# Feed-forward operands scaled by 1/rms once, and more weight pairs by seven half-block products

## The chip, the cores and the metric

The kernel runs on one core of a Trainium2 chip. The metric is the device time of one execution in microseconds (us), as the median of several runs. One further execution was profiled.

## The reference, cut to what matters

The program is a decoder trunk of two layers on 512 tokens of width 1024. Each layer is a feed-forward half step, a mixing block (attention and a gated MLP, not touched here) and a second feed-forward half step; a last norm ends it.

```
def rmsnorm(x, g):
    y = xf * lax.rsqrt(jnp.mean(xf * xf, axis=-1, keepdims=True) + EPS)
    return y * g
def swiglu(h, w_gate_up, w_down):
    g, u = jnp.split(h @ w_gate_up, 2, axis=-1)      # 1024 x 5632
    return (jax.nn.silu(g) * u) @ w_down             # 2816 x 1024
...
for l in range(DEPTH):                               # DEPTH = 2
    x = x + 0.5 * swiglu(rmsnorm(x, ffn1_norm[l]), ...)
    ...                                              # mixing block
    x = x + 0.5 * swiglu(rmsnorm(x, ffn2_norm[l]), ...)
```

All of it is float32.

## The kernel before

**Precision.** Every float32 operand is split into a high and a low part in the format that TensorE multiplies (fp32r): ScalarE copies it to the high part, VectorE subtracts to get the low part (`split`, line 352). A product is then three matmuls: high by high, high by low, low by high (`chain`, line 380). x is kept transposed, as eight tiles of 128 features by 512 tokens.

**The feed-forward** (`ffn`, line 577, four calls, here FFN1 to FFN4) walks over 22 pairs of weight blocks, j = 0 to 21: 128 gate columns and 128 up columns, each 1024 deep. The pairs come in four chunks, 0 to 5, 6 to 11, 12 to 17 and 18 to 21; after each chunk the down-projection of its hidden tiles runs (eight outputs of 128, 18 matmuls each for a chunk of six).

**A plain pair** (`pair_plain`) is 2 outputs x 8 depth blocks x 3 matmuls = 48 matmuls of 512 columns. **A pair of seven** (`pair_seven`) sees the same product as 2 x 2 blocks (gate and up; the two halves of the depth; the two halves of the tokens) and makes seven block products instead of eight, with sums of blocks as operands, as Strassen and Winograd have it: 7 x 4 depth blocks x 3 = 84 matmuls of 256 columns. It needs sums of the weights (tile `S`, three VectorE instructions per pair) and sums of the tokens' operands (`norm_sums`, line 420: n1, n2, t3, t4, once per feed-forward and depth block q, split into the tiles `Th` and `Tl`), and puts the results together on VectorE (tile `TT`, in the buffer YB). `SEVEN` (line 31) says which pairs do so: two of every three, from j = 4 in FFN1 and from j = 3 in the others, below 21: 11 pairs in FFN1, 12 in FFN2 to FFN4, 47 in all.

**The norm.** The operands `xh`, `xl` are x times the gain only. 1/rms (tile `rbc`, copied from PSUM by VectorE in `norm_finish`) is known later, so the results are multiplied by `rbc`: two VectorE instructions in a plain pair, two GpSimd instructions in a pair of seven. GpSimd also multiplies silu(gate) by up in both.

**Buffers.** Split weights live in a ring of three units of 1024 columns (Fhi in WH, Flo in WL). A plain pair takes two units, a pair of seven three (blocks 11 and 12; s1 and s2; s4 and s3) and half a unit for block 22 (in VH and VL). With the units named by age, a pair of seven finds its first unit free when the pair before has used its first product blocks, its last one when that pair ends. `norm_sums` writes through one buffer `T32`, so one q must be split before the next is summed. The tiles `Th`, `Tl` lie in buffers RB6 to RB11 and VH.

**Order.** The whole program is recorded first (`Recorder`); `order` then puts each engine's instructions in a fixed sequence by a list schedule with estimated costs, lowest index first among what is ready; weight loads and splits count as 100 places earlier (AHEAD). All instructions are issued by one line, 276, so in the profile they are told apart by tile names.

Of the kernel before, what the change touches and what calls it, by code (L numbers as in the profile page):

```python
# [29 lines left out]

def SEVEN(j, begins):

    return j % 3 < 2 and (FIRST if begins else LATER) <= j < 21


NEG = -1e30
# [243 lines left out]
def trunk(ctx: ExitStack, tc, d):  # L280
# [25 lines left out]

    for tag, places, cols, dtype in (
            ("Xraw", [(W[0], 0), (W[1], 0)], 2048, F32), ("Fraw", units(W[0], W[1]), 1024, F32),
            ("S", [(W[2], 0)], 2048, F32), ("T32", [(W[3], 0)], 1024, F32), ("Txa", [(W[4], 0)], S, F32), ("Txb", [(W[4], 512)], S, F32), ("ss0", [(W[4], 1536)], S, F32),
            ("Fhi", units(*WH), 1024, F32R), ("Flo", units(*WL), 1024, F32R),  # L310
            ("F22h", halves(V[1])[:2], S, F32R), ("F22l", halves(V[1])[2:], S, F32R),
            ("raw", units(W[0], W[1])[:3], 1024, F32), ("whi", units(*WH), 1024, F32R), ("wlo", units(*WL)[:2], 1024, F32R),
            ("raw5", units(W[0], W[1])[:3] + units(W[3]), 1024, F32), ("wlo3", units(*WL), 1024, F32R),
            ("whi5", units(*WH, RB[0], RB[1]), 1024, F32R), ("wlo5", units(*WL, RB[2], RB[3]), 1024, F32R),
            ("U", [(W[2], 0)], 2048, F32), ("pA", halves(W[3]), S, F32), ("pB", halves(W[4]), S, F32),
            ("ga", halves(W[1])[2:] + [(G, 0)], S, F32), ("diagh", [(WL[2], 0)], S, F32R), ("diagl", [(WL[2], 512)], S, F32R)):
        rec.over(tag, places, cols, dtype)
# [31 lines left out]
    def f(ap):  # L349
        return ap.bitcast(F32)  # L350
# [43 lines left out]
    def norm_begin(gidx):  # L394
        st["g"] = gains[:, gidx * KD:(gidx + 1) * KD]
        st["xh"], st["xl"] = [None] * KD, [None] * KD
        st["Th"], st["Tl"] = [None] * 4, [None] * 4
        st["s"] = None

    def norm_square(k):  # L400
# [10 lines left out]
    def norm_operand(k):  # L411
# [5 lines left out]
        act(xh, x[:, k, :], AF.Copy, scale=g)  # L417
        vec.scalar_tensor_tensor(xl, x[:, k, :], g, f(xh), op0=ALU.mult, op1=ALU.subtract)

    def norm_sums(q):  # L420

        t, xa, xb = rec.tile("T32", [P, 1024]), rec.tile("Txa", [P, S]), rec.tile("Txb", [P, S])
        act(xa, x[:, q, :], AF.Copy, scale=st["g"][:, q:q + 1])
        act(xb, x[:, q + 4, :], AF.Copy, scale=st["g"][:, q + 4:q + 5])
        n1, n2, t3, t4 = (t[:, n * 256:(n + 1) * 256] for n in range(4))
        vec.tensor_tensor(n1, xa[:, 0:256], xa[:, 256:512], op=ALU.subtract)
        vec.scalar_tensor_tensor(n2, xb[:, 256:512], -1.0, n1, op0=ALU.mult, op1=ALU.subtract)
        vec.tensor_tensor(t3, xb[:, 256:512], xa[:, 256:512], op=ALU.subtract)
# [82 lines left out]
        nb[0] += 1  # L511
        return bank(nb[0] % 6, "ps_gu")

    def pair_plain(w):
        out = []
        for p, q in (("21", "22"), ("11", "12")):
            ps = next_bank()
# [5 lines left out]
            chain(ps, ops)  # L523
            out.append(ps)
        g, u = tt("g"), tt("u")
        vec.tensor_tensor(g, out[0], rbc, op=ALU.mult)
        act(g, g, AF.Silu)
        vec.tensor_tensor(u, out[1], rbc, op=ALU.mult)
        pool.tensor_tensor(u, u, g, op=ALU.mult)
        return u  # L530

    def pair_seven(w):

        xh, xl, Th, Tl = st["xh"], st["xl"], st["Th"], st["Tl"]

# [18 lines left out]
        A, B, C, D = (next_bank() for _ in range(4))  # L554
        s1, TT = tt("s1")[:, 0:256], rec.tile("TT", [P, 1024])
        L, R = TT[:, 0:512], TT[:, 512:1024]
        times(A[:, 0:256], "11", "11")
        act(s1, A[:, 0:256], AF.Copy)
        times(B[:, 0:256], "12", "21")
        times(B[:, 256:512], "s2", "n2")  # L560
        vec.tensor_tensor(half(L), half(B), two(s1), op=ALU.add)
        times(C[:, 0:256], "s4", "22")
        times(C[:, 256:512], "s3", "t3")
        vec.tensor_tensor(half(R), half(C), two(L[:, 256:512]), op=ALU.add)
        times(D[:, 0:256], "22", "t4")
        vec.tensor_tensor(L[:, 256:512], D[:, 0:256], R[:, 256:512], op=ALU.add)
        times(A[:, 256:512], "s1", "n1")
# [657 lines left out]
```

## Time and profile before

| what | value |
|---|---|
| median of 3 runs | 2169.31 us (2168.56 to 2169.37) |
| the profiled execution: time, span | 2171.32 us, 2169.4 us |
| TensorE (PE) matmuls busy | 2139.0 us, 99% of the span |
| VectorE (DVE), ScalarE (ACT), GpSimd (POOL) busy | 70%, 47%, 17% |
| mean granted TensorE clock | 0.996 of 2.4 GHz |

The span runs from the first instruction to the last; the time has some 2 us around it. Busy shares are means over unlike stages: VectorE's 70% is far higher in some stretches. A matmul's row shows its own length, and matmuls overlap, so the pace of TensorE is read from the starts of successive ones.

### The profile page before, as it was taken

The numbers are of one execution on the slowest core, as the hardware profiler recorded it, in microseconds if no ns is written. First come the engines' busy times: TensorE is split into PE (matmuls) and PEld (weight loads), VectorE is DVE, ScalarE is ACT, GpSimd is POOL, SyncE is SP. The second block draws the span as 40 slices with busy tenths as digits, with TensorE's granted clock in tenths as the row PEclk, the third lists the DMA queues.
The fourth block names the chain that finished last, engine by engine and source line by source line (L and its number), as shares of the span: only waits on it lengthen the run. The fifth ranks groups of instructions, "written<-read, shape, count | busy, mean of one in ns | idle before, by whom it ended". The sixth has DMA issues, their size and how long they took to land.

```text
span 2169.4 us, 30061 instructions
## 1 busy us (share of the span) xinstructions
PE 2139.0 (99%) x11704; PEld 1849.9 (85%) x11704; DVE 1518.8 (70%) x2357; ACT 1011.9 (47%) x1635; POOL 379.6 (17%) x261
## 2 busy tenths in 40 slices
PE   8999999999999999999999999999999999999998
PEld 6898987888878889898888988878888788898986
DVE  7685767678885757585685775685888758585764
ACT  6343334676653533343453433357766436343434
POOL 2131322010000122231311413210100001231411
PEclk9999999999999999999999999999999999999999
DMA  5323333421113323323333232234111233323232
GB/s 191 115 88 107 91 100 114 149 62 47 59 59 124 104 89 106 109 88 107 89 100 113 88 115 87 91 109 160 49 58 50 69 107 97 112 86 114 85 101 68
DMA packets 65664, 209.25 MB, mean 96 GB/s; under 512 B 7793, under 2 KB 8305, under 8 KB 65521
## 3 DMA queue, kind: packets, MB, share of 16 engines
q1 hardware_dynamic: 65520, 207.32, 30.7%
q8 instruction: 92, 1.51, 0.3%
q14 instruction: 52, 0.42, 0.1%
HBM read 205.19 MB, written 2.10 MB: 96 GB/s over the span
## 4 chain that ended last, share of the span: by engine, by line
PE 93%; DVE 4%; ACT 2%; issue 1%; DMA 0%; SPq 0%; DVEq 0%; ACTq 0%
PE b L276 93%; DVE W L276 1%; DVE RB L276 1%; DVE WL L276 1%; DVE xl L276 1%; DVE x L276 1%; ACT WH L276 0%; ACT xh L276 0%; DMA x<-in_x_dram 0%; ACT t L276 0%; ACT L276 0%; ACT RB L276 0%; DVE t L276 0%; DVE YB L276 0%; DVE sm L276 0%
## 5 line engine op out<-in xcount | busy, mean ns | idle before, releaser
L276 ACT ACTIVATE WH<-W 128x1024 fp32r<-128x1024 f32 (+4 forms) x458 | 446.5, 976 | 636.5 <-PE b L276 553.4
L276 DVE TENSOR_TENSOR WL<-W,WH 128x1024 fp32r<-128x1024 f32 (+4 forms) x458 | 528.8, 1157 | 185.1 <-ACT WH L276 122.4
L276 PE MATMUL b<-xh,WH 128*128 128x512 f32 (+1 forms) x1716 | 608.5, 359 | 10.2 <-ACT xh L276 9.3
L276 PE MATMUL b<-xl,WH 128*128 128x512 f32 (+1 forms) x1716 | 608.5, 358 | 0.0
L276 PE MATMUL b<-RB,WH 128*128 128x512 f32 (+2 forms) x2270 | 579.7, 349 | 0.4
L276 PE MATMUL b<-xh,WL 128*128 128x512 f32 (+1 forms) x1716 | 568.8, 358 | 1.4 <-DVE WL L276 1.4
L276 PEld LDWEIGHTS b<-RB,WH 128*128 128x128 f32 x2270 | 397.9, 189 | 57.0 <-DVE x L276 2.1
L276 PE MATMUL b<-RB,WL 128*128 128x512 f32 (+1 forms) x1276 | 391.5, 341 | 0.0
L276 PEld LDWEIGHTS b<-xh,WH 128*128 128x128 f32 x1716 | 326.3, 190 | 56.6 <-ACT xh L276 9.7
L276 PEld LDWEIGHTS b<-xl,WH 128*128 128x128 f32 x1716 | 326.1, 190 | 45.5 <-DVE xl L276 1.1
L276 PEld LDWEIGHTS b<-xh,WL 128*128 128x128 f32 x1716 | 315.8, 190 | 46.6 <-DVE WL L276 2.3
L276 POOL TENSOR_TENSOR YB<-YB,rbc 128x512 f32<-128x512 f32 x94 | 168.6, 1812 | 671.3 <-DVE YB L276 671.3
L276 PEld LDWEIGHTS b<-RB,WL 128*128 128x128 f32 x1276 | 231.7, 190 | 27.3
L276 DVE SCALAR_TENSOR_TENSOR x<-b,x 128x512 f32<-128x512 f32 (+1 forms) x145 | 99.5, 686 | 166.6 <-PE b L276 166.6
L276 PE MATMUL b<-VH,WH 128*128 128x256 f32 (+1 forms) x426 | 136.3, 321 | 4.9 <-DVE W L276 4.9
L276 ACT ACTIVATE RB<-t 128x512 fp32r<-128x512 f32 (+3 forms) x120 | 67.7, 574 | 124.4 <-POOL t L276 112.5
L276 DVE TENSOR_TENSOR t<-b,rbc 128x512 f32<-128x512 f32 (+1 forms) x90 | 61.3, 687 | 91.6 <-PE b L276 91.3
L276 PE MATMUL b<-RB,RB 128*128 128x512 f32 (+4 forms) x478 | 124.8, 346 | 0.0
L276 POOL TENSOR_TENSOR t<-t,t 128x512 f32<-128x512 f32 x41 | 65.6, 1601 | 315.5 <-DVE t L276 253.0
L276 POOL TENSOR_TENSOR W<-W,t 128x512 f32<-128x512 f32 x35 | 49.3, 1409 | 403.0 <-ACT t L276 402.7
L276 DVE TENSOR_TENSOR RB<-t,RB 128x512 fp32r<-128x512 f32 (+3 forms) x120 | 77.0, 649 | 48.2 <-ACT RB L276 47.8
L276 DVE TENSOR_TENSOR W<-W 128x1024 f32<-128x1024 f32 (+3 forms) x87 | 97.7, 1122 | 5.6 <-ACT W L276 2.7
(161 smaller groups left out, 2443.7 us busy)
## 6 DMA issues: line engine op xcount, KB each, us to landing
W<-in_gu_dram SPq DMA_DIRECT2D x176, 512.0 KB, 3.7
W<-in_dn_dram SPq DMA_DIRECT2D x96, 384.0 KB, 3.1
W<-in_wA_dram SPq DMA_DIRECT2D x48, 512.0 KB, 3.5
W<-in_phi_dram SPq DMA_DIRECT2D x16, 512.0 KB, 4.5
W<-in_dn_dram SPq DMA_DIRECT2D x32, 256.0 KB, 2.7
W<-in_wo_dram SPq DMA_DIRECT2D x16, 512.0 KB, 3.5
W<-in_wv_dram SPq DMA_DIRECT2D x8, 512.0 KB, 4.2
W<-in_wu_dram SPq DMA_DIRECT2D x8, 512.0 KB, 5.3
```

Of the source, the lines that this page charges most:

```text
L276: getattr(self.real[engine], op)(*args, **kw)
```

## The change

1. `SEVEN` takes in j = 5 to 20 without a gap, and 3 (FFN2 to FFN4; 4 is plain) or 4 (FFN1; 5 is plain). These are 16 pairs in FFN1 and 17 in the others, 67 in all.
2. After pair 0, `norm_scaled` makes x times gain (ScalarE) times `rbc` (GpSimd) for all eight tiles, into eight buffers `xn`. `norm_sums` sums those, in place of two tiles `Txa`, `Txb` that ScalarE wrote for it from x.
3. At the first pair of seven, j = 3 or 4 (here "pair n0"), `norm_again` writes `xh` and `xl` anew from `xn`, in place: eight ScalarE copies, five VectorE and three GpSimd subtractions. From there on no result is multiplied by `rbc`. Pair n0 makes four of its products first, those that use only `Th` and `Tl`.
4. In plain pairs from n0 on, VectorE multiplies up by silu(gate) straight from PSUM; GpSimd has no part.

```
-    return j % 3 < 2 and (FIRST if begins else LATER) <= j < 21
+    return (FIRST if begins else LATER) <= j < 21 and j not in ((5,) if begins else (4,))
...
+    for k, place in enumerate(halves(W[3])[2:] + halves(W[4])[:3] + [(G, 0)] + rec.rings["tb"][0]):
+        rec.over(f"xn{k}", [place], S)
...
+    def norm_scaled(k):
+        st["xn"][k] = rec.tile(f"xn{k}", [P, S])
+        act(st["xn"][k], x[:, k, :], AF.Copy, scale=st["g"][:, k:k + 1])
+        pool.tensor_tensor(st["xn"][k], st["xn"][k], rbc, op=ALU.mult)
+    def norm_again(k):
+        st["xh"][k], st["xl"][k] = rec.tile(f"xh{k}", [P, S]), rec.tile(f"xl{k}", [P, S])
+        act(st["xh"][k], st["xn"][k], AF.Copy)
+        (vec if k < 5 else pool).tensor_tensor(st["xl"][k], st["xn"][k], f(st["xh"][k]), op=ALU.subtract)
     def norm_sums(q):
-        t, xa, xb = rec.tile("T32", [P, 1024]), rec.tile("Txa", [P, S]), rec.tile("Txb", [P, S])
-        act(xa, x[:, q, :], AF.Copy, scale=st["g"][:, q:q + 1])
-        act(xb, x[:, q + 4, :], AF.Copy, scale=st["g"][:, q + 4:q + 5])
+        t, xa, xb = rec.tile("T32", [P, 1024]), st["xn"][q], st["xn"][q + 4]
...
-    def pair_plain(w):
+    def pair_plain(w, scaled):
...
+        if scaled:
+            act(g, out[0], AF.Silu)
+            vec.tensor_tensor(u, out[1], g, op=ALU.mult)
+            return u
...
-        times(A[:, 0:256], "11", "11")
+        todo = {"B1": (B[:, 256:512], "s2", "n2"), "C1": (C[:, 256:512], "s3", "t3"), "A1": (A[:, 256:512], "s1", "n1"),
+                "D": (D[:, 0:256], "22", "t4"), "A0": (A[:, 0:256], "11", "11"), "B0": (B[:, 0:256], "12", "21"),
+                "C0": (C[:, 0:256], "s4", "22")}
...
+        if sums_first:
+            do("B1", "A1", "C1", "D")
+        do("A0")
         act(s1, A[:, 0:256], AF.Copy)
-        times(B[:, 0:256], "12", "21")
-        times(B[:, 256:512], "s2", "n2")
+        do("B0", "B1")
...
-        for v, r in ((L, rbc[:, 0:256]), (R, rbc[:, 256:512])):
-            pool.tensor_tensor(half(v), half(v), two(r), op=ALU.mult)
...
-                seven = SEVEN(j, gnext == 1)
+                seven, n0 = SEVEN(j, gnext == 1), FIRST if gnext == 1 else LATER
...
+                if j == n0:
+                    for k in range(KD):
+                        norm_again(k)
+                u = pair_seven(w, j == n0) if seven else pair_plain(w, j >= n0)
                 if j == 0:
+                    for q in range(4):
+                        norm_scaled(q)
+                        norm_scaled(q + 4)
                     for q in range(4):
                         norm_sums(q)
```

Outside pair n0 the order of the seven products is as before: A0, B0, B1, C0, C1, D, A1.

## Rows read from the trace of the kernel before

**Rows 1.** The page's head: span, busy time of each engine, the granted TensorE clock in 40 slices, and the chain of work that ended last by engine.

```profile
span 2169.4 us, 30061 instructions
PE 2139.0 (99%) x11704; PEld 1849.9 (85%) x11704; DVE 1518.8 (70%) x2357; ACT 1011.9 (47%) x1635; POOL 379.6 (17%) x261
PEclk9999999999999999999999999999999999999999
PE 93%; DVE 4%; ACT 2%; issue 1%; DMA 0%; SPq 0%; DVEq 0%; ACTq 0%
```

**Rows 2.** Busy time by stretch, for a pair of seven, the next pair of seven and the plain pair after them (pairs 6, 7 and 8 of FFN1): stretch, its length, then busy us (instructions) of PE, PEld, DVE, ACT, POOL, granted clock, DMA share, GB/s.

```profile
204.47:214.55 10.08, 10.08 (x86) 10.07 (x85) 8.60 (x11) 3.99 (x6) 0.14 (x1) 1.00 0.36 106
214.55:224.63 10.08, 10.08 (x87) 10.08 (x86) 9.94 (x11) 4.68 (x6) 5.25 (x3) 1.00 0.30 95
224.63:235.51 10.88, 10.88 (x50) 9.01 (x49) 7.50 (x9) 4.50 (x7) 4.80 (x3) 1.00 0.33 107
```

**Rows 3.** The waits of PE over the whole span: us in total, times, longest.

```profile
PE b L276 <- ACT xh L276: 9.3, 2, 8.1
PE b L276 <- DVE W L276: 7.2, 4, 2.7
```

**Rows 4.** Timeline of VectorE, then of ScalarE and GpSimd, while PE runs pairs 6 and 7 of FFN1: start, length, what, and in brackets the idle time before it and what ended it.

```profile
206.57 1.23 DVE L276 TENSOR_TENSOR W<-W 128x1024 f32<-128x1024 f32 x1
207.83 0.69 DVE L276 TENSOR_TENSOR W<-W,W 128x512 f32<-128x512 f32 x1
208.44 1.22 DVE L276 TENSOR_TENSOR WL<-W,WH 128x1024 fp32r<-128x1024 f32 x1
209.58 0.68 DVE L276 TENSOR_TENSOR W<-W,W 128x512 f32<-128x512 f32 x1
...
212.77 1.22 DVE L276 TENSOR_TENSOR WL<-W,WH 128x1024 fp32r<-128x1024 f32 x1 [0.21 <-ACT WH L276]
213.91 0.42 DVE L276 TENSOR_TENSOR YB<-b,YB 128x256 f32<-128x256 f32 x1
214.24 0.68 DVE L276 TENSOR_TENSOR VL<-W,VL 128x512 fp32r<-128x512 f32 x1
214.84 0.68 DVE L276 TENSOR_TENSOR YB<-YB,b 128x512 f32<-128x512 f32 x1
215.60 1.57 DVE L276 TENSOR_TENSOR WL<-W,WH 128x1024 fp32r<-128x1024 f32 x1
...
214.51 1.06 ACT L276 ACTIVATE WH<-W 128x1024 fp32r<-128x1024 f32 x1 [0.81 <-PE b L276]
```

**Rows 5.** Timeline of GpSimd and VectorE where two instructions meet (and one of GpSimd that meets none), and the row of VectorE's multiplications by `rbc` from the view of that tile (shortest, median and longest, in ns).

```profile
231.67 1.29 POOL L276 TENSOR_TENSOR t<-YB 128x512 f32<-128x512 f32 x1 [0.74 <-ACT YB L276]
236.57 2.24 POOL L276 TENSOR_TENSOR t<-t,t 128x512 f32<-128x512 f32 x1 [3.61 <-DVE t L276]
...
236.43 1.23 DVE L276 TENSOR_TENSOR WL<-W,WH 128x1024 fp32r<-128x1024 f32 x1
237.69 2.20 DVE L276 TENSOR_TENSOR W<-W 128x1024 f32<-128x1024 f32 x1
...
L276 DVE TENSOR_TENSOR t<-b,rbc x90: 667/691/692, 33.4 to 2134.0; 128x512 f32<-128x512 f32 x82, 64x496 f32<-64x496 f32 x8
```

**Rows 6.** Busy time by stretch at the start of each of the four feed-forwards, from the end of the copy of `rbc` to the start of pair n0; columns as in rows 2.

```profile
33.40:56.10 22.70, 22.70 (x102) 18.77 (x101) 21.71 (x30) 13.98 (x18) 3.60 (x3) 1.00 0.38 120
743.20:764.10 20.90, 20.90 (x93) 17.28 (x93) 17.58 (x24) 11.86 (x16) 3.46 (x2) 1.00 0.37 124
1095.20:1119.05 23.85, 23.85 (x106) 19.72 (x106) 23.00 (x32) 13.02 (x17) 2.64 (x2) 1.00 0.36 124
1815.60:1838.60 23.00, 23.00 (x104) 18.99 (x102) 19.00 (x27) 11.36 (x16) 2.93 (x2) 1.00 0.35 115
```

**Rows 7.** Timeline of VectorE around the start of FFN2: a low part `Tl` before `rbc`, the copy of `rbc`, a sum of `norm_sums`, the last `Tl`, and the low part of pair n0's s1 and s2; then the ScalarE row of the last `Th`.

```profile
736.94 1.22 DVE L276 TENSOR_TENSOR RB<-W,RB 128x1024 fp32r<-128x1024 f32 x1
...
742.52 0.69 DVE L276 COPY rbc<-b 128x512 f32<-128x512 f32 x1 [0.31 <-PE b L276]
...
751.29 0.42 DVE L276 TENSOR_TENSOR W<-W 128x256 f32<-128x256 f32 x1
751.63 0.42 DVE L276 SCALAR_TENSOR_TENSOR W<-W,W 128x256 f32<-128x256 f32 x1
...
753.17 1.23 DVE L276 TENSOR_TENSOR VH<-W,RB 128x1024 fp32r<-128x1024 f32 x1
...
759.59 1.23 DVE L276 TENSOR_TENSOR WL<-W,WH 128x1024 fp32r<-128x1024 f32 x1
...
752.08 1.06 ACT L276 ACTIVATE RB<-W 128x1024 fp32r<-128x1024 f32 x1 [1.81 <-DVE W L276]
```

**Rows 8.** Timeline of GpSimd: five instructions on 512 columns back to back, at a time when VectorE works too; and its groups over the whole span (count, busy us, mean ns).

```profile
13.80 8.60 POOL L276 TENSOR_TENSOR W<-W,t 128x512 f32<-128x512 f32 x5 [12.69 <-ACT t L276]
...
L276 POOL TENSOR_TENSOR YB<-YB,rbc 128x512 f32<-128x512 f32 x94 | 168.6, 1812 | 671.3 <-DVE YB L276 671.3
L276 POOL TENSOR_TENSOR t<-YB 128x512 f32<-128x512 f32 x47 | 69.6, 1482 | 36.1 <-ACT YB L276 36.1
```

**Rows 9.** Where the sums of FFN2 run before its start: ScalarE's wait for them, and the wait of PE that follows.

```profile
723.77 0.72 ACT L276 ACTIVATE W<-x,gains 128x512 f32<-128x512 f32 x1 [2.19 <-DVE W L276]
...
731.08 0.50 PE L276 MATMUL b<-xh,WH 128*128 128x512 f32 x1 [0.23 <-ACT WH L276]
```

More of the change, by code (lines that the diff above doesn't have):

```diff
@@ L308, in trunk @@
             ("Xraw", [(W[0], 0), (W[1], 0)], 2048, F32), ("Fraw", units(W[0], W[1]), 1024, F32),
-            ("S", [(W[2], 0)], 2048, F32), ("T32", [(W[3], 0)], 1024, F32), ("Txa", [(W[4], 0)], S, F32), ("Txb", [(W[4], 512)], S, F32), ("ss0", [(W[4], 1536)], S, F32),
+            ("S", [(W[2], 0)], 2048, F32), ("T32", [(W[3], 0)], 1024, F32), ("ss0", [(W[4], 1536)], S, F32),
             ("Fhi", units(*WH), 1024, F32R), ("Flo", units(*WL), 1024, F32R),
@@ L396, in norm_begin @@
         st["xh"], st["xl"] = [None] * KD, [None] * KD
-        st["Th"], st["Tl"] = [None] * 4, [None] * 4
+        st["Th"], st["Tl"], st["xn"] = [None] * 4, [None] * 4, [None] * KD
         st["s"] = None
@@ L530, in pair_plain, with pair_seven @@
         return u
-    def pair_seven(w):
+    def pair_seven(w, sums_first):
         xh, xl, Th, Tl = st["xh"], st["xl"], st["Th"], st["Tl"]
@@ L556, in pair_seven, with do @@
         L, R = TT[:, 0:512], TT[:, 512:1024]
-        times(A[:, 0:256], "11", "11")
+        todo = {"B1": (B[:, 256:512], "s2", "n2"), "C1": (C[:, 256:512], "s3", "t3"), "A1": (A[:, 256:512], "s1", "n1"),
+                "D": (D[:, 0:256], "22", "t4"), "A0": (A[:, 0:256], "11", "11"), "B0": (B[:, 0:256], "12", "21"),
+                "C0": (C[:, 0:256], "s4", "22")}
+        def do(*names):
+            for n in names:
+                if n in todo:
+                    times(*todo.pop(n))
+        if sums_first:
+            do("B1", "A1", "C1", "D")
+        do("A0")
         act(s1, A[:, 0:256], AF.Copy)
-        times(B[:, 0:256], "12", "21")
-        times(B[:, 256:512], "s2", "n2")
+        do("B0", "B1")
         vec.tensor_tensor(half(L), half(B), two(s1), op=ALU.add)
-        times(C[:, 0:256], "s4", "22")
-        times(C[:, 256:512], "s3", "t3")
+        do("C0", "C1")
         vec.tensor_tensor(half(R), half(C), two(L[:, 256:512]), op=ALU.add)
-        times(D[:, 0:256], "22", "t4")
+        do("D")
         vec.tensor_tensor(L[:, 256:512], D[:, 0:256], R[:, 256:512], op=ALU.add)
-        times(A[:, 256:512], "s1", "n1")
+        do("A1")
         vec.tensor_tensor(half(R), half(R), two(A[:, 256:512]), op=ALU.add)
-        for v, r in ((L, rbc[:, 0:256]), (R, rbc[:, 256:512])):
-            pool.tensor_tensor(half(v), half(v), two(r), op=ALU.mult)
         u = tt("u")
@@ L582, in ffn @@
             for j in range(c0, c1):
-                seven = SEVEN(j, gnext == 1)
+                seven, n0 = SEVEN(j, gnext == 1), FIRST if gnext == 1 else LATER
                 w = first.pop() if first else pair_split(pair_load(gu[l, j]), seven)
-                u = (pair_seven if seven else pair_plain)(w)
+                if j == n0:
+                    for k in range(KD):
+                        norm_again(k)
+                u = pair_seven(w, j == n0) if seven else pair_plain(w, j >= n0)
                 if j == 0:
+                    for q in range(4):
+                        norm_scaled(q)
+                        norm_scaled(q + 4)
                     for q in range(4):
@@ L590, in ffn @@
                 lo = rt(2 * (j % 6) + 1, "hl")
-                split(h, lo, u)
+                act(h, u, AF.Copy)
+                vec.tensor_tensor(lo, u, f(h), op=ALU.subtract)
                 hh.append(h)
```

## The prediction, as it was put on record

> **What bounds the kernel now.** I read the head of the page first. TensorE's matmuls fill 99% of the span at full clock (2.4 GHz), and the chain that ended last runs 93% over TensorE [rows 1]. So only two things can pay: fewer TensorE microseconds, or fewer waits. The list of PE's waits says that few are left: the longest groups are 9.3 us (the program's start) and 7.2 us in all [rows 3]. Then I cut out three neighbouring pairs of one feed-forward: TensorE is busy without a gap, 10.08 us for a pair of seven and 10.88 us for a plain pair [rows 2]. That is 84 matmuls at 0.120 and 48 at 0.2267 us. VectorE is off the path here, but look at its column: 9.94 of 10.08 us while a pair of seven follows a pair of seven, 7.50 beside a plain pair. So the question is whether VectorE, and GpSimd beside it, let TensorE keep its pace when the plain pairs in between are gone, and when FFN starts carry more.
>
> **TensorE's work.** 67 pairs of seven in place of 47 (the group of their 47 silu products counts them) [rows 8]: 20 x (10.88 - 10.08) = **-16.0 us** [rows 2]. Nothing else on TensorE changes. If VectorE holds TensorE to a slower pace, the gain is gone when the 16 pairs of FFN1 take on average (11 x 10.08 + 5 x 10.88) / 16 = 10.33 us each.
>
> **The lock between VectorE and GpSimd.** A GpSimd multiplication that started at 236.57, while VectorE was in an instruction that ended at 237.66, took 2.24 us in place of 1.29; VectorE's next one, from 237.69, took 2.20 in place of 1.23 [rows 5]. The two work in turn: GpSimd holds the way from 237.66 to 238.81, 1.15 us, and nothing overlaps. VectorE's multiplications by `rbc`, one input in PSUM, are never stretched (667 to 692 ns) [rows 5]. The Trainium skill (SBUF — State Buffer, Who interferes with whom) says the same: a VectorE instruction with two SBUF inputs and a GpSimd instruction that reads SBUF exclude each other for their whole length, and whichever starts first blocks the other. The trace agrees.
>
> **Long rows of seven.** VectorE's cost of one pair, by the steps from start to start [rows 4]: three low parts of weights at 1.14 (3.42), the first `S` sum 1.26, two more at 0.60 (1.2), the low part of block 22 0.60, four combinations (three at 0.60, one at 0.33: 2.13), the low part of the result 0.60. Sum 9.2 us. GpSimd's two multiplications by `rbc` go; its product with silu stays, 1.15 us of lock. It comes due some 1.8 us into the next pair, when VectorE has only two-SBUF work at hand, so I charge it in full: 10.35 us against 10.08, 0.27 us behind per pair. There is slack: the last unit of weights comes free as a pair ends (214.55), ScalarE takes 1.06 us from 214.51, and VectorE's low part from 215.60 would end near 216.8 without GpSimd [rows 4]. It is wanted after two products and four matmuls, 2.88 + 0.48 us into the pair, at 217.9. That leaves 1.1 us. Runs of seven are at most six long (6 to 11, 12 to 17), since the down-projections let VectorE catch up, and have five such passages: 5 x 0.27 = 1.35, or 0.25 us late. I take 0.5 us for each of the eight runs, **+4 us**; below it 0, above it, if VectorE also idles 0.4 us per passage behind a blocked head of its queue, (5 x 0.67 - 1.1) x 8 = 18 us.
>
> **The start of each feed-forward.** Before, half of `norm_sums` ran ahead of `rbc` (`Tl` at 736.94 against `rbc` at 743.2) [rows 7]. Now all of it waits for `rbc` and for eight GpSimd multiplications. Three ways to time the last `Tl` after `rbc`:
> - No contention: two multiplications at 1.3, then four rounds through the one buffer `T32`. A round is four sums at 0.34, `Th` 1.06, `Tl` 1.14 and hand-overs, 4.0 us [rows 7]. 2.6 + 16 = 18.6 us.
> - Everything in turn: 16 sums (5.4), four `Tl` (4.6), four low parts of weights that TensorE needs by then (4.6), `S` for pair n0 (2.4), and nine GpSimd multiplications (eight and pair 0's own) at 1.15 (10.4): 27.4 us.
> - GpSimd under load takes 8.60 / 5 = 1.72 us each [rows 8]: nine take 15.5; then two rounds of 4.0 and a low part in the way, 24.7, say **25**. I take this, as its row is the one with both engines at work.
>
> TensorE wants it 1.1 us into pair n0 (ninth and tenth matmul). With the windows [rows 6] that is at 23.8, 22.0, 24.95 and 24.1 us. Late at 25: 1.2 + 3.0 + 0.05 + 0.9 = **+5.2 us**. Bounds: 0, and at 27.4 (FFN1 has a second GpSimd product and a result to split, +1.7) 5.3 + 5.4 + 2.5 + 3.3 = 16.5 us. Nothing else is ready for TensorE then: later pairs need the rewritten `xh`. So a late `Tl` is a true stall.
>
> **Writing xh and xl anew.** `xh` of block k is free when pair n0 - 1 has passed it in its second chain, the last 5.4 us. Eight ScalarE copies fit there (ScalarE has half its time free [rows 6]). The four products ahead cover 4 x 1.44 = 5.76 us. In them VectorE owes s4 and s3's low part (1.14), block 22 (0.6) and at worst four `xl` (2.4), with four GpSimd holds (4.6) in turn: 8.7 us against 4.7 left after `Tl`. So 0 to 4 us each; a stall for `Tl` just before gives the same instructions time, so I take 0.25 each, **+1 us**.
>
> **At nothing.** The dropped `Txa` and `Txb` free ScalarE of a 2.19 us wait before FFN2, but PE lost only 0.23 us there [rows 9]; bound -0.5 over two such places. ScalarE's eight extra copies lie in its idle half. Chunks that now end in a pair of seven keep the same tail (combination, silu, GpSimd, split) that a plain pair has. DMA is untouched: the same weights.
>
> **Sum.** -16.0 + 4 + 5.2 + 1 = -5.8 us. The profiled execution took 2171.32 us (span 2169.4); that gives 2165.5. The median of the runs lies 2.0 us below it: **2163.5 us**.
>
> **Rivals.**
> 1. *Everything hides* (0.25). Rows 2 speak for it: at 9.94 busy us VectorE did not stop TensorE, though GpSimd had 5.25 us there. Then -16 and 0 to 4 us of stalls: 2153 to 2157.
> 2. *VectorE becomes the bound in the long rows* (0.22). For it: 10.35 against 10.08. Against: the 1.1 us of slack, and runs of six. At the upper end of 18 us with little at the starts: -16 + 18 = about +2, with half of it -5; 2165 to 2173, no change that can be told.
> 3. *The lock eats the gain at the starts* (0.20): slower. Place: between `rbc` and pair n0. Price: 16.5 us by the strict turn-taking, up to 4 for `xl`, 4 in the rows of seven: -16 + 24.5 = +8, 2177 us. It decides once a start costs more than (16 - 5 + 4.3) / 4 = 3.8 us on average, that is `Tl` past 27.5 us or late `xl`. For it: VectorE was already busy 21.71 of 22.70 and 23.00 of 23.85 us there [rows 6], and the change adds to it. Against: the work that pair n0 does not need can stand back. By the skill's rule alone (SBUF — State Buffer, same section) all of these holds add up.
>
> That the change does not do what it says is no rival: the instruction counts are fixed by the program.
>
> **How the numbers follow.** My forecast, stalls of 4 to 12 us in all, has 0.33 (2157 to 2165). Timings of this kernel tell 0.2%, 4.3 us, from no change. Faster: forecast and rival 1, 0.58. Same: rival 2, 0.22. Slower: rival 3, 0.20. Range 2153 (nothing stalls) to 2178 (rival 3's price); beyond it I leave the sum of both upper bounds (18 + 16.5) and a gain that the rows do not show. The forecast's own range is 2157 to 2165.
>
> **What the profile after would show.** PE at 11704 + 720 = 12424 matmuls; pairs of seven 10.08 us apart inside a run; `YB<-YB,rbc` gone and `t<-YB` at 67. If rows of seven bind, PE waits on VectorE's `WL` or ScalarE's `WH` inside runs, growing from the second to the sixth pair. If starts bind, one wait per feed-forward at pair n0, on VectorE's `Tl` (RB, VH, 128 x 1024), 1 to 5 us, largest in FFN2 and smallest in FFN3. If `xl` binds, a wait 5 us later. What would make me wrong: an order of the queues in which a VectorE instruction that waits for a late GpSimd one stands ahead of weights that TensorE needs, since every other start in my working assumes that the needed work goes first.

## The result: 1.4% slower, and the profile after

The changed kernel takes 2200.3 us (median of 4 runs, 2199.75 to 2200.89) against 2169.31 us (2168.56 to 2169.37) of the kernel before on the same chip: a ratio of 1.0143, 95% interval 1.0128 to 1.0158. The forecast was 2163.5 us, range 2153 to 2178. Sign and range were both missed.

The head of the page after, the chain that ended last by engine, and GpSimd's group of the silu products, to be set beside [rows 1, 8]:

```profile
span 2199.1 us, 31852 instructions
PE 2137.1 (97%) x12424; PEld 1879.9 (85%) x12424; DVE 1662.8 (76%) x2509; ACT 1067.4 (49%) x1727; POOL 270.6 (12%) x203
...
PE 80%; DVE 15%; issue 3%; ACT 1%; DMA 0%; DVEq 0%; POOL 0%; SPq 0%; ACTq 0%
...
L276 POOL TENSOR_TENSOR t<-YB 128x512 f32<-128x512 f32 x67 | 101.1, 1509 | 992.1 <-ACT YB L276 992.1
```

The change did what it says: 12424 matmuls, 67 pairs of seven, no product of `YB` with `rbc`. But VectorE's share of the last chain went from 4% to 15%. The waits of PE say where (us in total, times, longest; before, the list began with 9.3 and 7.2 [rows 3]):

```profile
PE b L276 <- DVE WL L276: 14.6, 11, 3.7
PE b L276 <- ACT xh L276: 10.5, 2, 9.5
PE b L276 <- DVE xl L276: 7.5, 6, 2.1
PE b L276 <- DVE W L276: 5.7, 3, 2.7
PE b L276 <- ACT WH L276: 4.5, 1, 4.5
PE b L276 <- ACT RB L276: 3.9, 3, 1.5
```

To see the place, I cut the same stretch out of both traces for each feed-forward: from the end of the copy of `rbc` to the start of the first down-projection. It holds the same pairs from pair 1 on in both kernels, since up to j = 5 one pair (FFN1) or two (the others) are of seven either way; how much of pair 0 lies behind `rbc` can differ. First before, then after; columns as in [rows 2]:

```profile
33.37:77.07 43.70, 43.70 (x233) 37.86 (x232) 35.54 (x45) 23.01 (x30) 10.21 (x7) 1.00 0.33 100
743.22:795.19 51.97, 51.97 (x310) 46.44 (x308) 39.07 (x48) 24.61 (x32) 15.87 (x9) 1.00 0.31 96
1095.22:1150.18 54.96, 54.96 (x323) 48.91 (x321) 45.52 (x58) 26.38 (x34) 14.78 (x9) 1.00 0.31 97
1815.64:1869.66 54.02, 54.02 (x319) 48.12 (x317) 40.49 (x51) 24.08 (x32) 15.34 (x9) 1.00 0.30 93
```

```profile
33.87:91.07 57.20, 48.86 (x233) 40.95 (x232) 48.91 (x54) 25.63 (x35) 25.81 (x16) 0.91 0.25 76
750.66:816.40 65.74, 58.63 (x320) 51.60 (x319) 58.19 (x64) 28.17 (x39) 25.25 (x15) 0.92 0.22 69
1110.86:1176.38 65.52, 58.73 (x323) 51.38 (x322) 57.63 (x63) 27.44 (x38) 25.14 (x15) 0.95 0.30 92
1837.55:1902.92 65.37, 58.08 (x320) 50.94 (x319) 58.17 (x64) 28.00 (x39) 25.42 (x15) 0.95 0.23 69
```

The starts are longer by 13.5, 13.8, 10.6 and 11.4 us, **49.2 us** in all. PE was never idle there before; now it is, for 8.3, 7.1, 6.8 and 7.3 us (length less busy time), 29.5 us in all, and its granted clock falls below 1. VectorE's busy time in the four rose from 160.6 to 222.9 us. Set against the shortest row of the same form, some 42 of these 62 us are rows that take longer than they need, waiting their turn, as will be seen; the rest is work that lay outside the cut before or is new. I call the sum of 49.2 us "the start loss" and give it for each experiment, by the same cut. Some 2.5 us of it are not lost but moved: in FFN2 `rbc` now comes earlier against TensorE's work, so that ten more matmuls of 512 columns (x320 against x310) lie behind it, and one more in FFN4.

The rest of the change went well. From down-projection to down-projection, the chunks that became six pairs of seven (6 to 11 and 12 to 17), and then the chunk 18 to 21, in FFN1 after:

```profile
91.07:184.88 93.81, 93.63 (x650) 87.62 (x649) 74.07 (x89) 36.73 (x49) 7.63 (x5) 1.00 0.33 103
184.88:278.36 93.48, 93.40 (x650) 87.56 (x649) 73.79 (x88) 38.32 (x51) 8.86 (x6) 1.00 0.33 102
278.36:352.17 73.81, 73.81 (x446) 66.29 (x445) 46.51 (x57) 26.78 (x35) 7.20 (x12) 1.00 0.32 98
```

Before, the three took 94.76, 94.76 and 74.58 us. Two and one more pairs of seven, at 0.8 us each, ask for 93.16, 93.16 and 73.78. So a long row (six pairs of seven one after another) costs 0.3 to 0.65 us, not more. The twelve chunks after the first ones gained 12.8 us. The remaining stretches took 6.7 us less, and the traces show where most of that comes from. The 2.5 us that moved behind `rbc` are missing here. And the kernel before has two stretches at half clock (1.2 GHz), in the first mixing block and just ahead of FFN3, where the changed kernel has full clock (columns as in [rows 2]; then the wait of TensorE ahead of the second stretch):

```profile
463.94:467.35 3.41, 3.41 (x12) 2.83 (x11) 3.35 (x6) 2.15 (x4) 0.58 (x1) 0.50 0.00 0
1088.58:1091.99 3.41, 3.41 (x10) 2.63 (x9) 1.34 (x6) 3.38 (x5) 0.00 (x0) 0.50 0.27 105
...
1087.20 1.05 PE L276 MATMUL b<-ones,W 128*128 128x1 f32 x8 [1.11 <-DVE W L276]
```

Matmuls of 512 columns step by 0.43 us there, not 0.227, which costs some 1.5 us in each. No kernel of this study touches the first mixing block itself; from the end of FFN1's down-projection to `rbc` it took 376.5 to 380.2 us among them, and the three at 376.5 to 376.6, the changed kernel among them, are without such a stretch. Ahead of FFN3 the difference goes with the change: from the start of FFN2's last down-projection to `rbc`, all nine kernels whose sums wait for `rbc` take 33.6 to 33.7 us, and the five whose sums begin before it 34.4 to 35.9. Sum: 49.2 - 12.8 - 6.7 = +29.7 us, the difference of the spans (2199.1 - 2169.4).

**Inside one start.** PE's stalls at the start of pair n0 in FFN2, with the idle time before each in brackets:

```profile
778.38 0.58 PE L276 MATMUL b<-RB,WL 128*128 128x256 f32 x1 [3.69 <-DVE WL L276]
...
779.52 0.58 PE L276 MATMUL b<-VH,WH 128*128 128x256 f32 x1 [0.34 <-DVE VH L276]
...
782.69 0.58 PE L276 MATMUL b<-RB,WH 128*128 128x256 f32 x1 [1.52 <-ACT RB L276]
...
791.23 0.39 PE L276 MATMUL b<-xl,WH 128*128 128x256 f32 x1 [1.55 <-DVE xl L276]
```

It is not one stall for the last `Tl`, but several in a row, the first of them for the low part of pair n0's own weights. VectorE and then GpSimd in that time (start, length, what; brackets are idle time before it):

```profile
749.97 0.69 DVE L276 COPY rbc<-b 128x512 f32<-128x512 f32 x1 [1.43 <-PE b L276]
...
756.19 2.31 DVE L276 TENSOR_TENSOR WL<-W,WH 128x1024 fp32r<-128x1024 f32 x1
758.43 1.51 DVE L276 SCALAR_TENSOR_TENSOR W<-W,W 128x256 f32<-128x256 f32 x1
759.86 1.51 DVE L276 TENSOR_TENSOR W<-W,W 128x256 f32<-128x256 f32 x1
761.29 1.52 DVE L276 SCALAR_TENSOR_TENSOR W<-W,W 128x256 f32<-128x256 f32 x1
...
766.15 1.21 DVE L276 TENSOR_TENSOR RB<-W,RB 128x1024 fp32r<-128x1024 f32 x1
...
769.28 0.42 DVE L276 TENSOR_TENSOR W<-G,W 128x256 f32<-128x256 f32 x1
...
776.35 1.98 DVE L276 TENSOR_TENSOR WL<-W,WH 128x1024 fp32r<-128x1024 f32 x1
...
783.27 2.31 DVE L276 TENSOR_TENSOR VH<-W,RB 128x1024 fp32r<-128x1024 f32 x1
```

```profile
759.61 1.47 POOL L276 TENSOR_TENSOR W<-W,rbc 128x512 f32<-128x512 f32 x1
761.05 1.48 POOL L276 TENSOR_TENSOR tb<-tb,rbc 128x512 f32<-128x512 f32 x1
762.49 1.48 POOL L276 TENSOR_TENSOR W<-W,rbc 128x512 f32<-128x512 f32 x1
```

While GpSimd multiplies, the two engines alternate, one instruction each. A sum of 256 columns takes 1.51 us, when GpSimd is done 0.42 (769.28). The eight multiplications end at 765.7, 15.0 us after `rbc`, but the first of four `Tl` only then begins (766.15), the others follow 5 to 6 us apart, and the last is ready at 785.6, 34.9 us after `rbc`. In those 34.9 us VectorE is idle for 0.46 us.

### The profile page after: what moved, and what is told of

It is laid out like the page before. It is cut to its first block, busy times and chain, and to the rows that moved or that the text cites. A ratio compares the mean times of both kernels' runs of the same rounds, so it can differ in the third digit from the quotient of the medians.

```text
span 2199.1 us, 31852 instructions
## 1 busy us (share of the span) xinstructions
PE 2137.1 (97%) x12424; PEld 1879.9 (85%) x12424; DVE 1662.8 (76%) x2509; ACT 1067.4 (49%) x1727; POOL 270.6 (12%) x203
## 3 DMA queue, kind: packets, MB, share of 16 engines
q1 hardware_dynamic: 65520, 207.32, 29.4%
## 4 chain that ended last, share of the span: by engine, by line
PE 80%; DVE 15%; issue 3%; ACT 1%; DMA 0%; DVEq 0%; POOL 0%; SPq 0%; ACTq 0%
PE b L276 80%; DVE W L276 5%; DVE WL L276 4%; DVE YB L276 2%; DVE RB L276 2%; DVE t L276 1%; DVE xl L276 1%; ACT RB L276 0%; DMA x<-in_x_dram 0%; DVE VH L276 0%; ACT WH L276 0%; DVE x L276 0%; ACT L276 0%; DVE VL L276 0%; ACT t L276 0%
## 5 line engine op out<-in xcount | busy, mean ns | idle before, releaser
L276 PE MATMUL b<-RB,WH 128*128 128x512 f32 (+1 forms) x2630 | 656.4, 342 | 8.4 <-ACT WH L276 4.5
L276 PE MATMUL b<-xh,WH 128*128 128x256 f32 (+1 forms) x1636 | 546.4, 341 | 11.2 <-ACT xh L276 10.5
L276 PE MATMUL b<-xl,WH 128*128 128x256 f32 (+1 forms) x1636 | 547.6, 341 | 7.6 <-DVE xl L276 7.5
L276 PE MATMUL b<-xh,WL 128*128 128x256 f32 (+1 forms) x1636 | 508.3, 341 | 3.0 <-DVE WL L276 3.0
L276 PE MATMUL b<-RB,WL 128*128 128x256 f32 (+1 forms) x1516 | 453.7, 335 | 12.0 <-DVE WL L276 11.6
L276 PEld LDWEIGHTS b<-xh,WH 128*128 128x128 f32 x1636 | 311.0, 191 | 44.5 <-ACT xh L276 10.9
L276 POOL TENSOR_TENSOR t<-YB 128x512 f32<-128x512 f32 x67 | 101.1, 1509 | 992.1 <-ACT YB L276 992.1
L276 DVE TENSOR_TENSOR W<-W 128x1024 f32<-128x1024 f32 (+2 forms) x91 | 135.2, 1487 | 5.2 <-POOL W L276 2.1
L276 PEld LDWEIGHTS b<-VH,WH 128*128 128x128 f32 x546 | 105.9, 194 | 13.9 <-DVE W L276 5.7
L276 DVE TENSOR_TENSOR W<-W,W 128x512 f32<-128x512 f32 (+1 forms) x149 | 109.3, 733 | 3.0
L276 PE MATMUL b<-RB,VL 128*128 128x256 f32 x670 | 109.7, 286 | 0.0
```

The source lines that it names most:

```text
L276: getattr(self.real[engine], op)(*args, **kw)
```

## The experiments

Where no interval is given, a kernel ran once; executions of the kernel before lie up to some 6 us apart (2167.83 to 2174.20), so a difference of a few us between single runs says nothing.

Theory A: VectorE's queue between `rbc` and pair n0 is full, and GpSimd's eight multiplications take the way to SBUF from it in turn. Theory B: it is the waiting for the scaled tiles (the multiplications, then four rounds of sums through one `T32`), whatever the engines' load. (The expectation of the first experiment puts B as too much work on VectorE, lock or not.) Theory C: rewriting `xh` and `xl` in place sets the time.

### VectorE multiplies in place of GpSimd

```
-        pool.tensor_tensor(st["xn"][k], st["xn"][k], rbc, op=ALU.mult)
+        vec.tensor_tensor(st["xn"][k], st["xn"][k], rbc, op=ALU.mult)
```

> The eight multiplications of xn by rbc run on VectorE instead of GpSimd; nothing else is changed. Measured so far: from the copy of rbc to the first down-projection the four feed-forwards take 13.5, 13.8, 10.6 and 11.4 us more than in the kernel before, 49.2 us in all. Theory A (turn-taking): in FFN2 six of the first sums are stretched from 0.42 to about 1.5 us, each behind a GpSimd multiplication, so that the first Tl comes 16 us after rbc. On VectorE a multiplication costs 0.6 us of its own and blocks nothing else: the start cost falls from 12.3 to about 7 us per feed-forward, 2175 to 2185 us. Theory B (VectorE has too much to do after rbc, lock or not): 8 x 0.6 = 4.8 us more of VectorE work per feed-forward, no gain or a loss: 2195 to 2215 us.

Measured: 2182.3 us, as A expected; the start loss falls from 49.2 to 31.4. Busy time in the first 15.04 us after `rbc` of FFN2, in the changed kernel and in this one:

```profile
750.66:765.70 15.04, 15.04 (x68) 12.41 (x67) 15.01 (x11) 5.92 (x8) 14.94 (x9) 1.00 0.25 88
```

```profile
748.55:763.59 15.04, 15.04 (x68) 12.41 (x67) 14.90 (x24) 6.22 (x7) 1.60 (x1) 1.00 0.24 88
```

VectorE is "busy" for 15 us in both, but gets through 11 instructions beside GpSimd's nine, and through 24, the eight multiplications among them, alone. The last `Tl` came 27.8 us after `rbc`, no longer 34.9. So giving VectorE more work made it finish sooner, which rules out that the count of VectorE's work alone decides. It doesn't yet tell turn-taking from waiting, since the eight multiplications also end sooner here, 8.4 us after `rbc` and not 15.0. 31 us of loss remain.

### Without the rewriting, and without the multiplications

```
-                if j == n0:
-                    for k in range(KD):
-                        norm_again(k)
...
+    vec.tensor_scalar(gains, gains, 0.01, None, op0=ALU.mult)
```

> The rewriting of xh and xl (norm_again) is left out, so pairs from n0 on use operands that were never scaled; the gains are made smaller by a factor of 100 in one small instruction so that the numbers stay finite. The output is not the reference's. Theory C (the rewriting is a second stall: in FFN1 PE waits 0.2, 2.05 and 0.59 us for xl, and the granted clock falls to half for 3.4 us just behind): the start cost falls by 4 to 6 us per feed-forward, 2176 to 2184 us. Theories A and B (the sums are late): the wait ahead of the first product stays, 2190 to 2197 us.

```
-        pool.tensor_tensor(st["xn"][k], st["xn"][k], rbc, op=ALU.mult)
...
+    vec.tensor_scalar(gains, gains, 0.01, None, op0=ALU.mult)
```

> The multiplication of xn by rbc is left out, so neither the eight GpSimd instructions nor the wait of the sums for rbc is there, while the copies to xn, the sums, the rewriting and the list of pairs stay; the gains are made smaller by a factor of 100 so that the numbers stay finite. The output is not the reference's. Theories A and B (all of the loss comes from what waits for rbc): the start cost falls from 49.2 to 10 us or less in all, 2155 to 2162 us. Theory C (the rewriting): 15 to 25 us stay, 2168 to 2178 us.

Measured: 2187.8 us without the rewriting, start loss 35.5: the rewriting is worth 13.7 us, between what A and C expected. And 2172.1 us without the multiplications, start loss 14.2: they are worth 35 us. The expectation of A and B (2155 to 2162) was too low: some of the sums run ahead of `rbc` again, and 14 us of loss stay even so, with waits of TensorE for `xl` (4.3 us) and for low parts of weights (3.6 us) at the starts. The parts overlap, so they don't add up to 49.

### The multiplications run, but nobody waits for them

The last run can't tell A from B: it took away both GpSimd's load and the wait for it. Here the load stays and the wait goes.

```
+    rec.over("idle", halves(YB), S)
...
-        pool.tensor_tensor(st["xn"][k], st["xn"][k], rbc, op=ALU.mult)
+        pool.tensor_tensor(rec.tile("idle", [P, S]), st["xn"][k], rbc, op=ALU.mult)
...
+    vec.tensor_scalar(gains, gains, 0.01, None, op0=ALU.mult)
```

> As e3_no_scaling (gains smaller by a factor of 100, sums and rewriting from operands that are not scaled, so that the sums wait for nothing but x), but GpSimd does the eight multiplications by rbc all the same, into a buffer that nobody reads (its output is not the reference's). The instructions are there, the wait for them is not. e3 has 14.2 us of loss at the four starts, the changed kernel 49.2. If the turn-taking of GpSimd and VectorE is the larger part of the difference (moving the multiplications to VectorE won back 17.8 us), the loss is 28 to 36 us here: 2185 to 2193 us. If the wait of the sums for rbc and the multiplications is, it stays at 14 to 19 us: 2172 to 2177 us.

Measured: 2195.6 us, start loss 39.8. Against 14.2 without them, eight instructions per feed-forward whose results are never read cost 25.6 us, 0.80 us each (25.6 / 32). That is more than expected, and it tells A from B: the two kernels differ by these instructions and their buffer alone. The wait for them, with the sums and `Tl` that it moves behind `rbc`, adds at most the other 9.4 us (49.2 - 39.8; some 2.5 of it is moved work). B explains the smaller part.

### Two buffers for the sums

```
-... ("T32", [(W[3], 0)], 1024, F32) ...
+... ("T32", [(W[3], 0), (YB, 0)], 1024, F32) ...
```

> The changed kernel with a second buffer for the sums (T32), so that the next block's sums need not wait for the split of the last. If the rounds through the one buffer set the time of the last Tl, as my working took it (a round of 4.0 us after GpSimd is done; the trace has 5 to 6), Tl comes 4 us or more earlier and the kernel gains 12 to 20 us: 2180 to 2187 us. If VectorE's queue and the turn-taking with GpSimd set it, the rounds only move: 2195 to 2201 us.

Measured: 2198.6 us, start loss 47.9. The copy of `rbc` in FFN2, the last `Tl` (its sums now in YB), and TensorE's first stall:

```profile
748.20 0.69 DVE L276 COPY rbc<-b 128x512 f32<-128x512 f32 x1 [1.44 <-PE b L276]
...
775.02 1.23 DVE L276 TENSOR_TENSOR VH<-YB,RB 128x1024 fp32r<-128x1024 f32 x1
...
777.43 0.58 PE L276 MATMUL b<-RB,WL 128*128 128x256 f32 x1 [4.49 <-DVE WL L276]
```

The last `Tl` did come earlier, 27.4 us after `rbc` in place of 34.9 (0.7, 7.6, 6.1 and 7.2 us earlier in the four feed-forwards), and the 12 to 20 us expected with it were not gained. In FFN2 TensorE now waited longer for a low part of weights, then for `xl`, and pair n0's last matmul started 44.9 us after `rbc` in place of 45.3. So the rounds through one buffer do hold up `Tl`, but the lateness of `Tl` does not set the time. What fits is the sum of all that VectorE owes before pair n0 can end.

### Is it the clock?

In and after the stalls the granted clock is at half (1.2 GHz): from 60.3 to 67.1 and 77.4 to 80.8 us in FFN1, 777.1 to 787.3 in FFN2, 1138.9 to 1145.7 in FFN3 and 1865.9 to 1872.8 in FFN4, 34.1 us in all. One matmul of 256 columns there steps by 0.21 us, not 0.12. By that step it is about 10 us of matmul time that the sum of the prediction did not have. Here 18 matmuls, whose results are not used, run ahead of pair n0 to fill the first stall.

```
+                if j == n0:
+                    for _ in range(18):
+                        pe.matmul(bank(6, "fill"), lhsT=st["Th"][0][:, 0:P], rhs=st["Th"][0][:, 0:S], start=True, stop=True)
```

> The changed kernel with 18 matmuls of 512 columns (4.1 us at full clock) of no use ahead of pair n0 in each feed-forward, on a tile that is ready early, into a PSUM bank that is idle there. TensorE works while it would wait. If half of the clock during and after the waits is a cost of its own (by the trace 9.9 us of the 49.2, in matmuls that run at 1.2 GHz), it falls away: 2187 to 2192 us. If the time is set by VectorE's queue alone, whatever TensorE does meanwhile, the total stays within 3 us of 2199; if the extra matmuls do not fit into the waits, it rises by up to 16 us.

Measured: 2211.8 us, slower still; of the three cases it is the last. PE in FFN1, the filler where the stall of 4.5 us had been, and a later stall:

```profile
57.58 4.24 PE L276 MATMUL b<-RB 128*128 128x512 f32 x18
...
75.17 0.58 PE L276 MATMUL b<-xl,WH 128*128 128x256 f32 x1 [2.73 <-DVE xl L276]
```

Full clock came back behind the filler (256 columns step by 0.12 us at 64.3), and yet this start took 1.0 us longer than without it: the wait for `xl` grew from 2.05 to 2.73 us, and half clock came later, from 73.6 to 80.4. In the other three starts the filler added 2.3 to 2.6 us. In all four together 27.3 us still ran at half clock, in place of 34.1. So this run shows that filling TensorE's first wait gains nothing while VectorE is late; it doesn't show what the half clock costs, since most of it stayed.

### Were the long rows of seven in danger?

The forecast charged them little, and they cost little. To see what that owes to the scaling, here is the kernel before with the new list of pairs alone (results still multiplied by `rbc` on GpSimd).

```
-    return j % 3 < 2 and (FIRST if begins else LATER) <= j < 21
+    return (FIRST if begins else LATER) <= j < 21 and j not in ((5,) if begins else (4,))
```

> The kernel before with the new list of pairs alone (67 of seven, up to six in a row); the results are still multiplied by rbc, by GpSimd in pairs of seven, and nothing waits for rbc that did not before. It tells whether the long rows needed the scaling at all. If each GpSimd instruction costs VectorE what it costs on average in the kernel before (0.43 us), a pair needs 9.2 + 3 x 0.43 = 10.5 us of VectorE: -16 + about 7 = 2160 us, faster than both. If all three hold VectorE up in full (9.2 + 3 x 1.15 = 12.65 us), each passage loses 2.6 us less 1.1 of slack once: eight runs at 11.8 us, -16 + 94, 2240 to 2250 us.

Measured: 2221.3 us, ratio 1.0235 (1.0218 to 1.0252), between the two expected cases. The starts are fine (43.7, 53.1, 55.7 and 54.0 us), but each chunk of six pairs of seven takes 100.4 to 101.7 us, on average 7.6 over the 93.16 that the matmuls ask for. A stretch of 3.4 us at half clock in each of these chunks is part of that. Where GpSimd's two multiplications of a pair meet a low part of VectorE (1.73 us in place of 1.21) and then a weight sum, and TensorE waits for the low part:

```profile
132.34 3.91 POOL L276 TENSOR_TENSOR YB<-YB,rbc 128x512 f32<-128x512 f32 x2 [5.63 <-DVE YB L276]
...
133.38 1.73 DVE L276 TENSOR_TENSOR WL<-W,WH 128x1024 fp32r<-128x1024 f32 x1
135.14 2.19 DVE L276 TENSOR_TENSOR W<-W 128x1024 f32<-128x1024 f32 x1
...
135.16 0.39 PE L276 MATMUL b<-RB,WL 128*128 128x256 f32 x1 [0.90 <-DVE WL L276]
```

Scaling the operands does what long rows need: it saves 7 us in each of eight chunks. It pays for that at the starts.

### Where VectorE has time to spare

If the price is a full VectorE between `rbc` and pair n0, a later n0 should lower it, as the sums get more pairs to hide behind. From pair 6 on (60 pairs of seven), and with 5, 5 in place of 6, 6 from pair 5 on (64):

```
-FIRST, LATER = 4, 3
+FIRST, LATER = 6, 6
...
-    return (FIRST if begins else LATER) <= j < 21 and j not in ((5,) if begins else (4,))
+    return (FIRST if begins else LATER) <= j < 21
```

> The same method, but with pair n0 = 6 in every feed-forward: all six pairs of the first chunk are plain, pairs 6 to 20 are of seven (60 pairs in place of 67, 47 before). The sums and the rewriting have the rest of the first chunk and its down-projection (32 us) to be done in. Theories A, B and C alike, as far as the loss is lateness at pair n0: the 49.2 us are gone, 7 x 0.8 = 5.6 us of TensorE work come back: 2199 - 49 + 6 = 2156 us, faster than the kernel before by 0.6%. If instead the loss lies in the long rows of seven themselves, it stays above 2180 us.

> Pair n0 = 5 in every feed-forward, then all pairs to 20 of seven: 64 pairs, and two pairs (10.88 us each) more time for the sums than the changed kernel gives in FFN2 to FFN4, one in FFN1. If lateness of the sums is the cause, it is covered (Tl came up to 12 us late), and what stays is the rewriting, 0 to 2.5 us per feed-forward: 2165.7 - 4 x 0.8 + 0 to 10 = 2162 to 2172 us. If the loss goes with a first pair of seven in the first chunk, wherever it stands, 2190 us or more.

And both again with VectorE multiplying, as in the first experiment:

> As e8_from_pair_five (the pairs of seven from pair 5 on, 2170.8 us), but VectorE multiplies the eight tiles by rbc, as in e1_scale_on_vector. If what is left at the starts of e8 (5.5 us of waits and 2.3 us at half clock, all in FFN1) is the turn-taking of GpSimd and VectorE, FFN1's start loses some 4 to 7 us and the time is 2164 to 2167 us. If it is that the needed work stands behind other work in VectorE's own queue, whoever multiplies, nothing changes: 2169 to 2172 us.

> As e4_from_chunk_two (from pair 6 on, 2165.7 us), but VectorE multiplies the eight tiles by rbc. In e4 PE waits 1.0 us in all at the starts, so there is nothing to take back: if turn-taking costs only where VectorE has no time to spare, the time stays within 2 us, 2164 to 2168 us. If the turn-taking costs in itself wherever it lies, the time falls by 5 us or more, to 2160 us or less.

| pairs of seven from | GpSimd multiplies | VectorE multiplies |
|---|---|---|
| 4 (FFN1), 3 (others): the change | 2200.3 us, 1.0143 | 2182.3 us |
| 5 | 2170.8 us, 1.0004 (0.9994 to 1.0013) | 2167.7 us, 0.9990 (0.9982 to 0.9999) |
| 6 | 2165.7 us, 0.9977 (0.9968 to 0.9987) | 2164.2 us, 0.9975 (0.9966 to 0.9984) |

The ratios are to the kernel before on the same chip. The gain from taking GpSimd out falls from 18 to 3 to 1.5 us as n0 moves back (by the intervals the last is not clear of nothing): turns cost where VectorE has no time to spare. From pair 6 on, PE hardly waits at the starts (45.5, 56.0, 56.7 and 56.0 us; less the plain pairs that stand in place of pairs of seven, 0.8 in FFN1 and 1.6 in the others, a start loss of 4 us in all, most of it FFN2's moved matmuls). From pair 5 on, FFN1 still does: it lost 7.8 us, of which VectorE as multiplier took back only 1.4 (to the end of the first down-projection, as some of its matmuls run ahead of pair 5's last ones there). So what is left there is mostly VectorE's own queue. Both kernels from pair 6 on are faster than the kernel before, by a quarter of a percent, and than the change. They are what is left of the idea: some 5 of its 16 us. The 2156 us expected from pair 6 on were not reached. The 13 added pairs ask for 10.4 us; 3 of them go in the first long rows, which begin with pair n0 and take 94.2 to 94.3 us, 0.7 to 0.8 more than the second ones.

### Two sets of operands

Last, a try to keep both: the early pairs of seven of the kernel before, with unscaled operands, and a second set of scaled sums made beside the first down-projection.

```
-    return (FIRST if begins else LATER) <= j < 21 and j not in ((5,) if begins else (4,))
+    return (j % 3 < 2 and (FIRST if begins else LATER) <= j < 6) or 6 <= j < 21
...
+                if j == n0 - 1:
                     for q in range(4):
                         norm_scaled(q)
                         norm_scaled(q + 4)
                     for q in range(4):
-                        norm_sums(q)
+                        norm_sums(q, True)
```

> Both methods, each where it is cheap: in the first chunk the pairs of seven of the kernel before (j = 4, or 3 and 4), with sums of unscaled operands made early as before and results multiplied by rbc; after pair 5 the operands are scaled, summed a second time and rewritten beside the first down-projection, and pairs 6 to 20 are of seven without rbc. 67 pairs of seven, as in the changed kernel. If starts that are late are all that the changed kernel lacks, this has e4's 2165.7 us less 7 x 0.8 = 5.6: 2160 us, and not over 2163. If the second set of sums beside the down-projection holds up pair 6 (VectorE owes 16 sums, 4 splits of 1024 columns and 5 low parts there, some 14 us in 32), 2 to 5 us more per feed-forward: 2168 to 2180 us.

Measured: 2224.9 us, ratio 1.0261 (1.0246 to 1.0277), the slowest of all and beyond both expected cases. The first down-projection was to hide the second set, and became the victim: it takes 45.4, 43.4, 42.7 and 41.6 us, where 144 matmuls take 32.4. Two of its stalls, VectorE's work ahead of the second, and the split that ends it:

```profile
87.49 0.73 PE L276 MATMUL b<-RB,WH 128*128 128x512 f32 x2 [2.08 <-ACT RB L276]
94.82 0.80 PE L276 MATMUL b<-RB,WH 128*128 128x512 f32 x1 [4.76 <-DVE RB L276]
```

```profile
85.22 5.15 DVE L276 TENSOR_TENSOR xl<-W,xh 128x512 fp32r<-128x512 f32 x3
90.29 2.28 DVE L276 TENSOR_TENSOR VH<-W,RB 128x1024 fp32r<-128x1024 f32 x1
...
94.08 0.69 DVE L276 TENSOR_TENSOR RB<-t,RB 128x512 fp32r<-128x512 f32 x1
```

The split of a hidden tile, which PE needs at once, stands behind `xl` and `Tl` for the next chunk, in a queue whose order is fixed.

## Why the prediction was wrong, step by step

- **TensorE's work, -16 us: right.** 12424 matmuls, and the twelve chunks after the first ones, where all 20 added pairs lie, gained 12.8 us. The other 3.2 us are the long rows' cost.
- **Long rows, +4 us: right.** 3.2 us, 0.3 to 0.65 per row where 0.5 was taken. In each of the eight rows TensorE is late at one or two places, ahead of a matmul that reads a low part of weights (WL), as the forecast had it. Rival 2 falls. That the same rows without the scaling cost 7.6 us each shows that the count of VectorE's time per pair (10.35 against 10.08 us) was close to the edge, and that one GpSimd instruction per pair is on the right side of it and three are not.
- **The start of each feed-forward, +5.2 us: the step that failed.** 49.2 us were lost there (46.7 without the moved matmuls). Two things were wrong. The first is the time of the last `Tl`: I took it at 25 us after `rbc`, with 27.4 as the upper end; it came at 29.4 in FFN1 and 34.6 to 34.9 in the others. GpSimd's part was timed rightly (15.5 taken, 15.0 measured). What came after was not: "then two rounds of 4.0 and a low part in the way" supposed that two of four rounds were done by then, but in FFN2 the first was just ending, and three more of 5 to 6 us followed. The upper end used the right model, everything in turn, with an incomplete list. The trace after shows what else VectorE did in those 34.9 us of FFN2: six products of plain results with `rbc` (6 x 0.6), two low parts of hidden tiles (1.2), block 22's low part (0.6), one `xl` (0.6), and two more turns of GpSimd (2.3). 27.4 + 3.6 + 1.2 + 0.6 + 0.6 + 2.3 = 35.7, about what was measured. All of these could have been listed from the program and the trace of before.
- **The second is the path, and it weighs more.** The sum lets pair n0 wait for the last `Tl` alone. With two sum buffers the last `Tl` came at 27.4 in FFN2, the upper end, for which the sum has 16.5 us at most; 47.9 were lost. TensorE waited for all that VectorE owed before pair n0 could end: low parts of weights, `Tl` and `xl`, in whatever order they stood.
- **The order of the queue.** I named as what would make me wrong a queue in which other work stands ahead of what TensorE needs. It was so: the first stall of pair n0 was for its own weights (the low part, 3.69 us, in FFN2; the high part, 4.5 us, in FFN1), which stood behind the sums, not for `Tl`.
- **Rewriting, +1 us: mis-sized.** It is worth 13.7 us (one run without it). That is within 0 to 4 us per feed-forward, but I took the low end because "a stall for `Tl` just before gives the same instructions time". It doesn't: VectorE was full during that stall, and GpSimd's three subtractions (784.8 to 790.6 in FFN2) took turns with the last `Tl`, the last low part and the `xl` of VectorE.
- **Rival 3** had the place and the mechanism, with a price of 16.5 + 4 us where 49.2 was lost. The price at which it decides, 3.8 us per start, was worked out rightly. In the chances it got 0.20, although [rows 6] show VectorE busy for 21.71 of 22.70 and 23.00 of 23.85 us. A shorter sum would have told the sign: all that the change adds to VectorE's queue after `rbc`, less its slack. In the trace of before, six, eleven, four and eight of the 16 sums and one, two, no and two of the `Tl` ran ahead of `rbc` (the forecast had half of them, which is FFN4's case). After it come these, five `xl` (3.0) and eleven GpSimd turns (12.65): at 0.34 and 1.14 each that is 18.8, 21.7, 17.0 and 20.7 us of VectorE's time. Against them stand VectorE's slack in [rows 6] (1.0, 3.3, 0.9 and 4.0 us) and the 5.8 us of the four products ahead: 12.0, 12.6, 10.3 and 10.9 us late, 46 in all. The starts lost 13.5, 13.8 (11.5 without the moved work), 10.6 and 11.4. This is worked out with the result known, and it is less good for the experiments: without the rewriting it gives 20 us, and 35.5 were lost.
- **At nothing.** The sums that no longer run ahead of `rbc` gave back 2.2 us ahead of FFN3, where the forecast had 0.5 at most for two such places: half clock after a wait of 1.1 us in the kernel before is gone.
- **The clock** was not in the sum at all. By the step of its matmuls the half clock took about 10 us; how much of that is on top of VectorE's lateness stays open.

On the lock itself the forecast used the right rule and didn't follow it through. The Trainium skill (SBUF — State Buffer, Who interferes with whom) has it that a VectorE instruction with two SBUF inputs and a GpSimd instruction that reads SBUF contend for an exclusive lock. The traces agree, with 1.51 us for a sum of 0.42. A chance of one in five was too little for a lock that [rows 5] had already shown.

## What to carry to other kernels

Before moving work to a point that everything waits for, list all that the engine has to do between that point and the last of the operands that are waited for, its own routine results included, and add the other engine's turns in full. An engine that is already 95% busy in that window, as VectorE was in FFN1 and FFN3, is late by nearly all that is added; its mean over the span (70% here) says nothing. And an instruction on a "free" engine isn't free if it takes turns with the busy one: taking the multiplications back to VectorE was faster by 18 us, and moving the same work to where VectorE has time made it nearly free.

## What the runs showed of the hardware

- GpSimd and VectorE alternate instruction by instruction while both have work, so the short VectorE instruction loses most: 0.42 to 1.51 us for 256 columns, 1.23 to 2.31 for 1024. Busy time counts the wait: 11 instructions filled the same 15 us as 24.
- Eight GpSimd multiplications whose results nobody reads cost 6.4 us per feed-forward at these starts, where VectorE is full; what they do to the granted clock is in it.
- During or soon after waits inside a kernel that was busy before, the granted clock stood at half for 3.4 to 10.2 us at a time: in the changed kernel's starts with waits of 2 to 4.5 us, in the kernel before also after one of 1.1 us (1088.6 to 1092.0). The step of a 256-column matmul was 0.21 us in place of 0.12, that of a 512-column one 0.43 in place of 0.227.
